# Seven-product steps for two more pairs of K tiles in in1 and o1, blocks opened with a classical step, and squares issued later

## The chip, the cores and the metric

One core of one Trainium2 chip runs the program; it is launched once per measurement. The metric is the device time of one execution in microseconds (us). The kernel before takes 1145.22 us (median of 3 runs, 1143.92 to 1145.31).

## The reference

One layer of an encoder trunk for 256 positions of width 2048, all in float32. What is computed, cut to its products:

```python
n = rmsnorm(h, norm_mix_w)
q_a, k_a, v_a, q_r, k_r, v_r, g_r = split(n @ w_in)     # seven sections of 1024 columns
attn = dilated_mixture_attention(q_a, k_a, v_a)         # 8 heads
ret = bidirectional_retention(q_r, k_r, v_r)            # 8 heads, per-head norm
ret = ret * silu(g_r)
h = h + concat(attn, ret) @ w_out                       # 2048 x 2048
n2 = rmsnorm(h, norm_ffn_w)
h = h + (silu(n2 @ w_gate) * (n2 @ w_up)) @ w_down      # 5632 hidden columns
y = rmsnorm(h, norm_final_w)
```

## The kernel before

**Products.** Each float32 product is made of three products in the format fp32r: an activation and a weight tile are each held as a high and a low half, and high by high, high by low and low by high are accumulated in PSUM (the accumulators beside TensorE). One such matmul has 128 rows of K and 512 columns. ScalarE (ACT) writes a weight tile's high half as a rounded copy, and VectorE (DVE) writes the low half as the difference; both go through the helpers at L156 and L159. A weight tile holds 128 by 1024 numbers and arrives as one DMA of 512 KB that SyncE (SP) issues.

**Blocks.** The program is a row of blocks. A block makes 1024 columns for all 256 positions, in four PSUM banks that are numbered 2, 3, 4 and 8. `in0` to `in6` are the input projection (L787 and L233), `o0` and `o1` the output projection, `gu0` to `gu10` gate and up side by side, and `d0_0`, `d0_1`, `d1_0`, `d1_1`, `d2_0` and `d2_1` the product with `w_down`, which comes after four, eight and eleven `gu` blocks.

**Steps.** A string in `ORDERS` says which steps a block takes and in which order. `C` is the classical step: one weight tile, 12 matmuls. A digit with a letter is one of seven products (Strassen's scheme), which treat two pairs of K tiles together: the letter `a` or `b` names the group, and each digit is 6 matmuls into the bank with that number. A group takes 42 matmuls and four weight loads (three at step 1, one at step 2), where four classical tiles take 48 matmuls. Beside the halves of its tile a seven-product step needs sums of weights: step 1 has VectorE add two loaded tiles into a tile called `rawt` (there is one of it) and GpSimd (POOL) issue an accumulating DMA of 512 KB into `raw12`; step 5 has VectorE add a third tile to `rawt`; step 2 issues another accumulating DMA, from `rawt` into `raw22` (helper `plus`, L178). Steps 3, 5, 6 and 7 also need sums of the activations, `sa_...`, which `pair_sums` makes on VectorE.

**Other letters.** `M` is `mid`: the products 1, 5, 6 and 7 are combined on VectorE into four tiles `part0` to `part3`, one for each quarter of the block's output; the banks 2, 3, 4 and 8 are added to them when their last matmul is done. In `o0` and `o1` the parts are added at `M` into the residual tiles `ht` by four accumulating DMAs of 256 KB on POOL (`add_parts`), and the banks follow as VectorE additions into `ht` (`end_out`). `H`, `T` and `N` are places for other work: `T` transposes (on TensorE, L365) what the block before has made, `H` scales or combines it, and `N` queues work.

**What sets the order.** Each engine runs its instructions in the order in which the program writes them; a manual dependency chains them (`ch`). A weight tile's halves are written three work steps ahead of their products (`AHEAD`), into five buffers `ws`. `later` is a list from which one entry is run behind each work step, `soon` a list that runs behind the next one. So work on VectorE, ScalarE or POOL that waits holds back whatever is written behind it on that engine.

**Around the change.** `sums_n1` queues, for the first two pairs of n1, three entries of `later` each: the sum of the two halves, the sums of its quarters and their halves. Behind them `measure_x` queues 11 entries that fetch x in eight pieces of 256 KB on POOL's queue (L442), and square each on ScalarE three entries later; the sums of these squares give the factor `r1` of the first norm, which `factor` computes on VectorE and POOL (L200 to L202). In the same way `square_ht` squares the eight pieces of `ht` after w_out into `sums_h`, and `gate(gu0)`, which is the `H` of `gu1`, begins with `factor(r2, sums_h)`: with `r2` ScalarE forms the Silu of the gate half and VectorE multiplies the up half (L162), and then `gu0` is transposed into `h2` (`pt_h`). `weighed` writes the halves of a transposed `n2` with the norm's gain, alternating between ScalarE and VectorE.

## Time and profile before

| what | value |
|---|---|
| time, median of 3 runs | 1145.22 us (1143.92 to 1145.31) |
| the profiled execution | 1148.03 us |
| its span, first to last instruction | 1146.2 us |
| granted TensorE clock, mean | 0.995 |
| TensorE (PE) busy | 1127.6 us, 98% |
| VectorE (DVE) busy | 924.2 us, 81% |
| ScalarE (ACT) busy | 681.9 us, 59% |
| GpSimd (POOL) busy | 106.5 us, 9% |

The profile is of one execution. The span is what lies between its first and its last instruction; the remaining 1.8 us of the execution lie around it. Names in the rows are the program's, without the numbers of their buffers: `p_in`, `p_o` and `p_gu` are PSUM banks, `ws_...` weight tiles in halves, `rawc`, `raw12`, `raw22` and `rawt` weight tiles as loaded or summed, `xs` the pieces of x, `pt_...` transposed tiles. "[1.57 <-ACT ws_gu L156]" says that the engine was idle for 1.57 us until an instruction of ScalarE at L156 on that tile released it.

The blocks start on TensorE at these times of the span: `in1` 50.2, `in2` 94.3, `in5` 245.6, `in6` 295.8, `o0` 344.1, `o1` 392.8, `gu0` 437.6, `gu1` 486.0, `gu2` 532.5.

### The profile page before, as it was taken

Reading aid. Unit: us, or ns where it says so; the run is one execution under the profiler, and the core shown is the slowest. Engines: PE = TensorE matmul, PEld = TensorE weight load, DVE = VectorE, ACT = ScalarE, POOL = GpSimd, SP = SyncE. Lnnn points to the kernel's source line nnn. Section 1 sums busy time; section 2 is a strip of 40 time slices with the busy share of each in tenths; the row PEclk is TensorE's granted clock in tenths of the full one; section 3 lists DMA queues with packets and bytes.
Section 4 is the critical chain, followed back from the end, with each engine's and each line's share of the span. In section 5 each row is a group of like instructions: output and inputs, shape, how many; then the busy total and the mean of one; then the engine's idle time right before and its main releaser. Section 6 shows DMA issues by size and latency. Waiting matters only on the chain.

```text
span 1146.2 us, 14428 instructions
## 1 busy us (share of the span) xinstructions
PE 1127.6 (98%) x5166; PEld 935.5 (82%) x5166; DVE 924.2 (81%) x1056; ACT 681.9 (59%) x841; POOL 106.5 (9%) x135
## 2 busy tenths in 40 slices
PE   9999999999999999989999999999999999999996
PEld 7888888888888887878888888888888888888885
DVE  5768876845566868699999878999989977999885
ACT  5675655754656555566666554666666555666653
POOL 0102000000001110010000022000001202000011
PEclk9999999999999999999999999999999999999999
DMA  8969654465588776678898899997898899989795
GB/s 279 308 195 313 209 168 148 150 217 169 174 272 245 218 211 196 208 211 246 261 254 245 258 272 257 284 269 232 251 288 237 229 317 264 277 259 276 240 232 152
DMA packets 78535, 272.03 MB, mean 237 GB/s; under 512 B 9088, under 2 KB 9088, under 8 KB 78464
## 3 DMA queue, kind: packets, MB, share of 16 engines
q1 hardware_dynamic: 61776, 220.76, 55.3%
q0 software_dynamic: 15968, 49.29, 23.1%
q10 hardware_dynamic: 720, 1.07, 0.3%
q8 instruction: 40, 0.66, 0.2%
q14 instruction: 31, 0.25, 0.1%
HBM read 223.90 MB, written 2.10 MB: 197 GB/s over the span
## 4 chain that ended last, share of the span: by engine, by line
PE 83%; DVE 6%; DMA 5%; issue 3%; ACT 2%; POOL 0%; SPq 0%; DVEq 0%; POOLq 0%; ACTq 0%
PE p_gu L233 35%; PE p_in L233 26%; PE p_d L233 13%; PE p_o L233 5%; DMA rawc_d<-in_w_st 2%; DMA rawc_gu<-in_w_st 2%; DVE ws_d L159 2%; DVE ws_gu L159 2%; PE pt_h L365 1%; DMA rawc_o<-in_w_st 1%; DVE ht L159 1%; ACT ws_gu L156 1%; DVE ws_o L159 1%; PE ps_sa L482 1%; PE ps_oa L493 1%
## 5 line engine op out<-in xcount | busy, mean ns | idle before, releaser
L233 PE MATMUL p_gu<-ws_gu,n 128*128 128x512 f32 x1482 | 353.1, 391 | 3.3 <-ACT ws_gu L156 2.6
L233 PEld LDWEIGHTS p_gu<-ws_gu,n 128*128 128x128 f32 x1482 | 278.8, 188 | 62.8 <-ACT ws_gu L156 3.7
L233 PE MATMUL p_in<-ws_in,n 128*128 128x512 f32 x1284 | 302.0, 391 | 1.2 <-ACT ws_in L156 1.1
L233 PEld LDWEIGHTS p_in<-ws_in,n 128*128 128x128 f32 x1284 | 238.2, 188 | 50.4 <-ACT ws_in L156 2.5
L159 DVE TENSOR_TENSOR ws_in<-rawc_in,ws_in 128x1024 fp32r<-128x1024 f32 (+1 forms) x107 | 129.1, 1213 | 62.2 <-ACT ws_in L156 61.3
L233 PE MATMUL p_d<-ws_d,h 128*128 128x512 f32 x708 | 167.9, 389 | 0.4 <-ACT ws_d L156 0.4
L159 DVE TENSOR_TENSOR ws_gu<-rawc_gu,ws_gu 128x1024 fp32r<-128x1024 f32 x113 | 137.8, 1221 | 29.4 <-ACT ws_gu L156 27.6
L233 PEld LDWEIGHTS p_d<-ws_d,h 128*128 128x128 f32 x708 | 132.8, 188 | 28.6 <-ACT ws_d L156 1.1
L156 ACT ACTIVATE ws_in<-rawc_in 128x1024 fp32r<-128x1024 f32 (+1 forms) x107 | 111.6, 1047 | 69.8 <-PE p_in L233 36.1
L156 ACT ACTIVATE ws_gu<-rawc_gu 128x1024 fp32r<-128x1024 f32 x113 | 118.7, 1055 | 56.6 <-DMA rawc_gu<-in_w_st 33.0
L233 PE MATMUL p_gu<-ws_gu,sa_n 128*128 128x512 f32 x504 | 129.3, 392 | 0.0
L233 PEld LDWEIGHTS p_gu<-ws_gu,sa_n 128*128 128x128 f32 x504 | 94.7, 189 | 19.3
L159 DVE TENSOR_TENSOR ws_gu<-raw_gu,ws_gu 128x1024 fp32r<-128x1024 f32 x84 | 102.5, 1220 | 2.2 <-ACT ws_gu L156 1.0
L156 ACT ACTIVATE ws_gu<-raw_gu 128x1024 fp32r<-128x1024 f32 x84 | 88.5, 1054 | 20.9 <-PE p_gu L233 18.5
L159 DVE TENSOR_TENSOR ws_d<-rawc_d,ws_d 128x1024 fp32r<-128x1024 f32 x54 | 65.8, 1221 | 19.1 <-ACT ws_d L156 18.4
L156 ACT ACTIVATE ws_d<-rawc_d 128x1024 fp32r<-128x1024 f32 x54 | 57.1, 1058 | 39.7 <-DMA rawc_d<-in_w_st 22.6
L156 ACT ACTIVATE ws_gu<-rawt_gu 128x1024 fp32r<-128x1024 f32 x42 | 44.3, 1055 | 56.7 <-DVE rawt_gu L159 38.8
L233 PE MATMUL p_d<-ws_d,sa_h 128*128 128x512 f32 x240 | 61.2, 390 | 0.0
L159 DVE TENSOR_TENSOR ws_gu<-rawt_gu,ws_gu 128x1024 fp32r<-128x1024 f32 x42 | 51.3, 1221 | 5.6 <-ACT ws_gu L156 5.6
L233 PEld LDWEIGHTS p_d<-ws_d,sa_h 128*128 128x128 f32 x240 | 44.8, 188 | 9.2
L159 DVE TENSOR_TENSOR ws_d<-raw_d,ws_d 128x1024 fp32r<-128x1024 f32 x40 | 48.8, 1220 | 0.5
L156 ACT ACTIVATE ws_d<-raw_d 128x1024 fp32r<-128x1024 f32 x40 | 42.2, 1055 | 10.5 <-PE p_d L233 9.1
(186 smaller groups left out, 1139.3 us busy)
## 6 DMA issues: line engine op xcount, KB each, us to landing
rawc_gu<-in_w_st SPq DMA_DIRECT2D x113, 512.0 KB, 5.0
rawc_in<-in_w_st SPq DMA_DIRECT2D x105, 512.0 KB, 4.2
raw_gu<-in_w_st SPq DMA_DIRECT2D x63, 512.0 KB, 5.3
rawc_d<-in_w_st SPq DMA_DIRECT2D x58, 512.0 KB, 5.0
raw_d<-in_w_st SPq DMA_DIRECT2D x30, 512.0 KB, 4.7
rawc_o<-in_w_st SPq DMA_DIRECT2D x26, 512.0 KB, 4.8
raw_gu<-raw_gu POOLq DMA_DIRECT2D x21, 512.0 KB, 6.9
raw_gu<-rawt_gu POOLq DMA_DIRECT2D x21, 512.0 KB, 5.3
```

Of the source, the lines that this page charges most:

```text
L156: ch(nc.scalar.activation(out, src, func, **kw))
L159: ch(nc.vector.tensor_tensor(out, x, y, op=op))
L233: ch(nc.tensor.matmul(self.bank(r), x[u], w[v], start=r not in self.begun, stop=self.left[r] == 0))
L365: ch(nc.tensor.transpose(pt[:, f, i * P:(i + 1) * P], t(i)[:, (2 * p + f) * P:(2 * p + f + 1) * P], ident))
L482: ch(nc.tensor.matmul(ps[:, i, :], a, b, start=n == 0, stop=n == 2))
L493: ch(nc.tensor.matmul(ps[:, f, :], a, b, start=i + n == 0, stop=i == 1 and n == 2))
```

## The change

1. `in1` takes a second group of seven products (order string below); its `H`, with the norm's factor and the scaling of `in0`, stands right behind `M`, and its two `T` stand behind one another. Its sums of n1 are made for four pairs where they were made for two, so that `sums_n1` queues twelve entries of `later` ahead of `measure_x`, where it queued six.
2. `in5` becomes a block of kind `in` (one group of seven products); the sums of the first two pairs of n1 are made a second time, by a hook `S` in `in3` and `in4`'s order string, which is filled in `in4`. What `in5` has made is then scaled in the `H` of `in6`.
3. `o1` takes a second group and begins with a classical step; the mixed activations' sums are made for four pairs.
4. `gu0` begins with a classical step.
5. The squares of `ht` are put behind three empty entries of `later` in each of `o0` and `o1`, and `factor(r2, sums_h)` is itself queued in `later` behind the last square, during `gu0`, where it stood at the start of `gate` in `gu1`.
6. `weighed` writes both of ScalarE's copies first, and then both of VectorE's differences.

TensorE gets 5132 matmuls and transposes where it had 5150: three groups more, of 6 matmuls less each. VectorE gets 57 instructions more and ScalarE 16.

```diff
@@ ORDERS @@
-KIND_IN = ("in0", "in1", "in", "in_c", "in_c", "in_c", "in_c")
+KIND_IN = ("in0", "in1", "in", "in_c", "in_c", "in", "in_c")
...
-    "in1": "1a 5a C 2a C 3a C C 6a C 7a M C H C C T C T 4a C C C",
+    "in1": "1a 5a C 2a C 3a C 6a 7a 1b C 4a 5b C 2b 6b C 7b M H C C T T 3b 4b",
     "in": "1a 5a H C 2a C T 3a C T C 6a C 7a M C C C 4a C C C C",
-    "in_c": "C H C T C T C C C C C C C C C C C C C",
+    "in_c": "C H C T C T C C C C C C C S C C C C C C",
     "out0": "1a 5a H C 2a T C 6a 7a M C 3a C 4a C C C C C C C C",
-    "out1": "1a 5a 2a C 3a C T 6a C 7a C M C 4a C T C C C C C C",
-    "gu_first": "1a 5a 2a C T C C T C 3a 6a C 7a C 4a M C C C C C C",
+    "out1": "C 1a 5a 2a C 3a T C C 6a C 7a 1b 4a 5b C 2b 6b C 7b M C T 3b 4b",
+    "gu_first": "C 1a 5a C 2a T C C C T C 3a 6a C 7a C 4a M C C C C",
@@ weighed @@
         for f in range(2):
             copy(to[:, f, 0, :], src[:, f, :], scale=w[:, f:f + 1])
+        for f in range(2):
             stt(to[:, f, 1, :], src[:, f, :], w[:, f:f + 1], to[:, f, 0, :].bitcast(F32), ALU.mult, ALU.subtract)
@@ sums_n1 @@
-    def sums_n1():
-        for p in range(2):
+    def sums_n1(to, n):
+        for p in range(n):
...
-            n1_sums.append(pair_sums(t, f"n1_{p}"))
+            to.append(pair_sums(t, f"n1_{p}"))
@@ attention @@
-            if j < 2:
+            if j < 4:
                 mixed_sums.append(pair_sums(o[0], f"ma{j}"))
@@ the loop over INPUT @@
-            hooks = {"N": [sums_n1, measure_x]}
+            hooks = {"N": [many((sums_n1, n1_sums, 4)), measure_x]}
...
-                hooks = {"H": [many(*([(factor, r1, sums_x)] if b == 1 else []), *([(scaled, prev, 0, 1)] if sec == 0 else []))],
+                hooks = {"H": [many(*([(factor, r1, sums_x)] if b == 1 else []), *([(scaled, prev, 0, 1)] if sec == 0 or half else []))],
...
+            if b == 4:
+                hooks["S"] = [many((sums_n1, n1_again, 2))]
+            end = end_take if b == 0 else end_share if "1a" in ORDERS[KIND_IN[b]] else end_scaled
@@ end_out @@
         tt(o, bank, o, ALU.add)
+        if not block.squares:
+            later.extend([lambda: None] * 3)
+        block.squares += 1
         later.append(lambda: square_ht(sums_h, block.q + n, i))
+        if block.q + block.squares == 6:
+            later.append(lambda: factor(r2, sums_h))
@@ gate @@
-        if block.first:
-            factor(r2, sums_h)
         for i in range(2):
```

The lines of the changed kernel stand one or more lower (L159 is L159 there too, L178 is L179, L233 is L234, L442 is L443). Three places where the order on an engine moves:

**In `in1`, POOL.** `xs00` to `xs31` are the eight pieces of x, `raw12` and `raw22` the accumulating DMAs of the seven products. Before:

```order
L442 DMA xs00_405<-in_x 128x512
L442 DMA xs01_426<-in_x 128x512
L178 DMA raw12_in1_430<-raw22_in1_432 128x1024
L442 DMA xs10_452<-in_x 128x512
L442 DMA xs11_470<-in_x 128x512
L442 DMA xs20_496<-in_x 128x512
L178 DMA raw22_in1_499<-rawt_in1_437 128x1024
L442 DMA xs21_512<-in_x 128x512
L442 DMA xs30_527<-in_x 128x512
L442 DMA xs31_549<-in_x 128x512
```

and changed:

```order
L179 DMA raw12_in1_439<-raw22_in1_441 128x1024
L179 DMA raw22_in1_507<-rawt_in1_446 128x1024
L443 DMA xs00_520<-in_x 128x512
L443 DMA xs01_534<-in_x 128x512
L443 DMA xs10_555<-in_x 128x512
L443 DMA xs11_568<-in_x 128x512
L443 DMA xs20_586<-in_x 128x512
L443 DMA xs21_598<-in_x 128x512
L179 DMA raw12_in1_603<-raw22_in1_605 128x1024
L443 DMA xs30_625<-in_x 128x512
L443 DMA xs31_640<-in_x 128x512
L179 DMA raw22_in1_683<-rawt_in1_610 128x1024
```

The first two pieces stood ahead of group a's DMAs and now stand behind both, and the last two stand behind group b's first DMA, in front of its second.

**In `in1`, ScalarE**, in the middle of the changed block (a `ws` row writes the high half of a weight tile, an `xs` row squares a piece of x):

```order
L156 ACTIVATE ws_in1_630<-rawc_in1_628 128x2x512
L156 ACTIVATE xs20_586,sums_x_93<-xs20_586 128x512
L156 ACTIVATE ws_in1_643<-raw22_in1_507 128x2x512
L156 ACTIVATE xs21_598,sums_x_93<-xs21_598 128x512
L156 ACTIVATE ws_in1_654<-rawt_in1_610 128x2x512
L156 ACTIVATE xs30_625,sums_x_93<-xs30_625 128x512
L156 ACTIVATE ws_in1_667<-rawc_in1_665 128x2x512
L156 ACTIVATE xs31_640,sums_x_93<-xs31_640 128x512
L156 ACTIVATE ws_in1_685<-raw22_in1_683 128x2x512
```

Before, all eight squares stood between the block's second and tenth tile; now the last of them, `xs31`, stands between its fourteenth and its fifteenth, and `xs30`'s stands in front of the fourteenth (`ws_in1_667`, the classical tile behind 5b).

**At the end of `o1`, VectorE**, from `mid` on, before:

```order
L159 TENSOR_TENSOR v_o1_3479<-part0_o1_3475,p6_o1_3404 128x512 [waits Activation_49]
L162 SCALAR_TENSOR_TENSOR part2_o1_3477<-p5_o1_3310,v_o1_3479 128x512 [waits DVE_49]
L159 TENSOR_TENSOR part1_o1_3476<-p7_o1_3445,v_o1_3479 128x512 [waits PE_49]
L159 TENSOR_TENSOR part3_o1_3478<-part2_o1_3477,p7_o1_3445 128x512 [waits DVE_49]
L159 TENSOR_TENSOR ws_o1_3491<-rawc_o1_3489,ws_o1_3491 128x2x512 [waits DMAHW6_49,Activation_49]
L159 TENSOR_TENSOR ws_o1_3508<-rawc_o1_3506,ws_o1_3508 128x2x512 [waits DMAHW7_49,Activation_49]
L159 TENSOR_TENSOR ws_o1_3519<-rawc_o1_3517,ws_o1_3519 128x2x512 [waits DMAHW1_49,Activation_49]
L159 TENSOR_TENSOR ws_o1_3554<-rawc_o1_3552,ws_o1_3554 128x2x512 [waits DMAHW2_49,Activation_49]
L159 TENSOR_TENSOR n2_1_0_3539<-o_n2_10_3540,n2_1_0_3539 128x2x256 [waits Activation_49]
L159 TENSOR_TENSOR n2_1_1_3548<-o_n2_11_3549,n2_1_1_3548 128x2x256 [waits Activation_49]
```

The four additions of banks into `ht` came only with gu0's fourth to sixth tiles there. Changed:

```order
L159 TENSOR_TENSOR v_o1_3681<-part0_o1_3677,p6_o1_3545 128x512 [waits Activation_49]
L162 SCALAR_TENSOR_TENSOR part2_o1_3679<-p5_o1_3413,v_o1_3681 128x512 [waits DVE_49]
L159 TENSOR_TENSOR part1_o1_3678<-p7_o1_3577,v_o1_3681 128x512 [waits PE_49]
L159 TENSOR_TENSOR part3_o1_3680<-part2_o1_3679,p7_o1_3577 128x512 [waits DVE_49]
L159 TENSOR_TENSOR ws_gu0_3693<-rawc_gu0_3691,ws_gu0_3693 128x2x512 [waits DMAHW2_49,Activation_49]
L159 TENSOR_TENSOR ht2_3483<-p2_o1_3382,ht2_3483 128x512 [waits DMASW2_49,PE_49]
L159 TENSOR_TENSOR ht3_3485<-p8_o1_3391,ht3_3485 128x512 [waits DMASW5_49,PE_49]
L159 TENSOR_TENSOR ws_gu0_3734<-rawc_gu0_3728,ws_gu0_3734 128x2x512 [waits DMAHW3_49,Activation_49]
L159 TENSOR_TENSOR rawt_gu0_3737<-rawc_gu0_3728,raw12_gu0_3730 128x1024 [waits DMAHW7_49]
L159 TENSOR_TENSOR ht3_3485<-p3_o1_3385,ht3_3485 128x512 [waits DMASW4_49,PE_49]
L159 TENSOR_TENSOR n2_1_0_3715<-o_n2_10_3716,n2_1_0_3715 128x2x256 [waits Activation_49]
L159 TENSOR_TENSOR n2_1_1_3724<-o_n2_11_3725,n2_1_1_3724 128x2x256 [waits Activation_49]
```

The rows carry the semaphores that they wait for; `DMASW` is one of POOL's DMAs. The additions into `ht` now stand two instructions behind `mid`, and `n2_1_0`, whose high and low halves gu0's first classical step multiplies, stands behind three of them.

More of the change, by code (lines that the diff above doesn't have):

```diff
@@ L410, in end_share @@
         tt(block.share[i, n], bank, block.share[i, n], ALU.add)
-    xt, n1, n1_sums = {}, [], []
+    xt, n1, n1_sums, n1_again = {}, [], [], []
     def fetch_x(p):
@@ L674, in encoder_layer @@
         if sections[0] is not None:
-            prev = Block(f"in{b}", KIND_IN[b], n1, n1_sums, end_take if b == 0 else end_share if b < 3 else end_scaled, hooks,
+            if b == 4:
+                hooks["S"] = [many((sums_n1, n1_again, 2))]
+            end = end_take if b == 0 else end_share if "1a" in ORDERS[KIND_IN[b]] else end_scaled
+            prev = Block(f"in{b}", KIND_IN[b], n1, n1_again if b > 2 else n1_sums, end, hooks,
                          opens=b == 0, early=b < 3)
@@ L707, in encoder_layer @@
         b = Block(f"o{nb}", f"out{nb}", mixed, mixed_sums, end_out, hooks, parts="mid")
-        b.q = 2 * nb
+        b.q, b.squares = 2 * nb, 0
     def gate(block):
-        if block.first:
-            factor(r2, sums_h)
         for i in range(2):
@@ L761, in encoder_layer @@
             b = Block(f"gu{fb}", kind, n2, n2_sums, end_share, hooks)
-            b.first = fb == 0
             def turn_h(b=b, h2=h2, s2=s2, keep=2 * (fb - lo) < s, fb=fb):
```

## The prediction, as made before the result was known

> **What bounds the kernel now.** I read the page first, then the list of waits of TensorE, then busy time in windows that are cut by blocks. The page's first part and the waits:
>
> ```profile
> PE 1127.6 (98%) x5166; PEld 935.5 (82%) x5166; DVE 924.2 (81%) x1056; ACT 681.9 (59%) x841; POOL 106.5 (9%) x135
> ...
> PE pt_h L365 <- DVE part_gu L162: 3.2, 3, 2.6
> PE p_gu L233 <- ACT ws_gu L156: 2.6, 2, 1.6
> PE p_in L233 <- ACT ws_in L156: 1.1, 2, 0.9
> PE p_gu L233 <- DVE ws_gu L159: 0.7, 1, 0.7
> PE p_o L233 <- ACT o_n L156: 0.5, 1, 0.5
> PE p_d L233 <- ACT ws_d L156: 0.4, 1, 0.4
> ```
>
> TensorE is busy 98% of the span, and all its waits for other engines come to some 10 us. So a matmul taken away is time taken away, as long as TensorE finds its next tile ready, and a new wait of it costs its full length. The windows are `in1`, `o1`, `gu0` and, for comparison, `gu2`, a block with two groups of seven products:
>
> ```profile
> 50.20:94.20 44.00, 44.00 (x203) 36.55 (x203) 30.07 (x32) 30.27 (x46) 4.17 (x6) 1.00 0.76 247
> 392.80:437.50 44.70, 44.21 (x203) 36.58 (x202) 32.94 (x48) 26.83 (x41) 3.54 (x5) 1.00 0.72 208
> 437.60:486.00 48.40, 46.14 (x204) 37.50 (x203) 34.74 (x40) 27.50 (x39) 2.50 (x3) 0.96 0.65 204
> 532.50:574.20 41.70, 41.70 (x189) 34.62 (x188) 40.58 (x49) 27.33 (x31) 3.44 (x4) 1.00 0.86 253
> ```
>
> The columns behind the window's length are busy PE, weight loads, DVE, ACT and POOL, then the granted clock. In `in1` and `o1` TensorE is without a gap, or nearly; `gu0` lost 2.3 us and ran at 0.96. A block with two groups asks 40.58 of 41.70 us of VectorE and still leaves TensorE no gap. VectorE has 30 to 33 us of work in `in1` and `o1`, so there is room for a second group on average; what decides is the order in which it and POOL's queue do their work.
>
> **The sum, term by term.** The rows of TensorE for the first four terms, from the chain of waits and the timeline:
>
> ```profile
> 376.61 27.25 PE p_o L233 x120
> 80.33 0.87 PE pt_q L365 x8
> ...
> 405.23 1.66 PE L233 MATMUL p_o<-ws_o,sa_ma 128*128 128x512 f32 x6 [0.49 <-ACT o_n L156]
> 442.05 0.73 PE L233 MATMUL p_gu<-ws_gu,n 128*128 128x512 f32 x2 [0.69 <-DVE ws_gu L159]
> 444.35 4.61 PE L233 MATMUL p_gu<-ws_gu,n 128*128 128x512 f32 x12 [1.57 <-ACT ws_gu L156]
> 495.53 0.33 PE L365 MATMUL pt_h<-ident,part_gu 128*128 128x128 f32 x1 [2.56 <-DVE part_gu L162]
> 496.19 1.76 PE L365 MATMUL pt_h<-ident,part_gu 128*128 128x128 f32 x7 [0.34 <-DVE part_gu L162]
> ```
>
> (1) *Matmuls.* 120 in 27.25 us is 0.227 us for one, 1.36 for a seven-product step and 2.73 for a classical one. Three groups more take 18 matmuls away: **−4.1**.
>
> (2) *o1's T.* Its 6a waited 0.49 for ScalarE, which was held by the copies of the transposed n2. Two classical steps now stand in between: **−0.5**.
>
> (3) *gu0's start.* `gu0` waited 0.69 and 1.57, and after that 12 matmuls took 4.61 instead of 2.73, at a granted clock that the window shows as 0.96. With a classical step first and no accumulating DMA needed at once, both waits and the slow stretch of 1.9 go: **−4.1**. What takes their place is term 8.
>
> (4) *gu1's gate.* The rows of VectorE, POOL and ScalarE there:
>
> ```profile
> 491.64 1.22 DVE L159 TENSOR_TENSOR ws_gu<-raw_gu,ws_gu 128x1024 fp32r<-128x1024 f32 x1
> 493.22 0.72 POOL L202 TENSOR_TENSOR r<-r,mhalf 128x2 f32<-128x2 f32 x1 [3.86 <-DVE r L201]
> 493.97 1.33 ACT L156 ACTIVATE part_gu<-part_gu,r 128x512 f32<-128x512 f32 x2 [6.58 <-POOL r L202]
> 494.73 1.41 DVE L162 SCALAR_TENSOR_TENSOR part_gu<-part_gu,r,part_gu 128x512 f32<-128x512 f32 x2 [1.59 <-ACT part_gu L156]
> ```
>
> With r2 known beforehand ScalarE, idle for 6.58 us, forms the Silus before VectorE is through with its tile at 492.86; the multiplications then start there and not at 494.73, 1.9 earlier. TensorE's wait of 2.56 shrinks to under one, and the 7 transposes behind it, 1.76 us where 8 took 0.87 elsewhere, gain 1.0: **−2.9** (−1 if the slow clock stays and half of the wait, −4 with the rest of it).
>
> (5) *in1, a new wait.* Here the order matters: on POOL the last two pieces of x now stand behind group b's first accumulating DMA, and that waits until VectorE has made group b's `rawt`. ScalarE's square of `xs30` stands in front of the high half of the classical tile behind 5b, so this tile waits for that fetch to land. The rows of `in1`, POOL, then ScalarE, and the times from issue to landing of the fetches at 47.6, at 55.1 and of the two at 27:
>
> ```profile
> 47.08 0.89 POOL L178 DMA_DIRECT2D raw_in<-raw_in  x1 [18.68 <-DVE rawt_in L159]
> 47.64 1.96 POOL L442 DMA_DIRECT2D xs<-in_x  x3
> 54.56 0.90 POOL L178 DMA_DIRECT2D raw_in<-rawt_in  x1 [4.96 <-DVE ws_in L159]
> 55.13 1.97 POOL L442 DMA_DIRECT2D xs<-in_x  x3
> ...
> 61.05 0.63 ACT L156 ACTIVATE xs<-xs 128x512 f32<-128x512 f32 x1 [1.75 <-DMA xs<-in_x]
> 61.67 1.04 ACT L156 ACTIVATE ws_in<-rawc_in 128x1024 fp32r<-128x1024 f32 x1
> ...
> DMA to landing us min/median/max: 6.8/7.0/8.2
> ...
> DMA to landing us min/median/max: 5.9/6.0/6.7
> ...
> DMA to landing us min/median/max: 3.9/4.0/4.0
> ```
>
> Up to 2a the two orders are alike, so `xs00` is issued where a piece was issued before, behind the DMA at 54.56, and its square starts at 61.05 as that one's did. From there a square and a high half take 0.62 + 0.95 = 1.57; 6a's and 7a's tiles go ahead and 1b's high half ends at 65.8. VectorE writes the low half (1.22) and adds `rawt` (as long, 1.14 start to start): 68.2. POOL issues the accumulating DMA at 68.5, and by the row at 47.64, 0.56 behind such a DMA and 6.8 to land, `xs30` is there 7.4 later, at 75.9. Square and high half: 77.6. TensorE starts `in1` at 50.2; nine seven-product steps and four classical ones, 23.2, bring it to that tile at 73.4. Wait: **+4.2**; with the fetch at 4.0, as at 27, 1.4; with 8.2, 5.6. An idle time of 2.3 in `gu0` was followed by the slow stretch, so I add the same **+1.9** (0 to 1.9).
>
> [...]
>
> (6) *The end of in1 and in2's start.* `M H C C T T 3b 4b` brings the scaling and four transposed halves together. Rows of ScalarE from the groups of 70 to 95:
>
> ```profile
> L156 ACT ACTIVATE part_in<-part_in,r 128x512 f32<-128x512 f32 x4 | 2.6, 711 | 3.7 <-POOL r L202 3.7
> L156 ACT ACTIVATE q<-pt_q 128x512 fp32r<-128x512 f32 x2 | 1.1, 576 | 0.0
> ```
>
> From the end of 7b: VectorE's `mid` and the factor 1.8, POOL 0.8, four scalings 2.6, two high halves 2.0 (7.2); VectorE's low half and `rawt` of in2's first group 2.5 (9.7); ScalarE's half of `rawt` 1.05, four transposed halves 2.3 and the first classical tile of `in2` 1.05 (14.1). TensorE wants that one after two classical steps, 16 transposes (1.7) and four seven-product steps: 12.6. That is 1.5 late; VectorE's low half, behind four additions, a sum and four halves more, is another 1.5 late: **+3.0** (0 to 4).
>
> (7) *in5.* Its second step uses sums that VectorE finishes behind `in4`'s scaled copies: **+0.4** (0 to 1); the rest of the moved work lies in blocks where VectorE has 30 us of 44.
>
> (8) *o1's end, the largest term.* VectorE's additions of banks 2 and 8 into `ht2` and `ht3` now stand two instructions behind `mid`, and the second waits for the fourth accumulating DMA. Behind it stand gu0's 1a tile, its `rawt`, another addition and then the low half of `n2_1_0`, which gu0's first step multiplies. Rows of `o1` now, VectorE, POOL, and the landing of those DMAs; the last row is that of the same three DMAs at 1124, of `d2_1`:
>
> ```profile
> 416.27 0.68 DVE L159 TENSOR_TENSOR part_o<-part_o,p_o 128x512 f32<-128x512 f32 x1
> 416.87 2.36 DVE L159 TENSOR_TENSOR ws_o<-rawc_o,ws_o 128x1024 fp32r<-128x1024 f32 x2
> ...
> L178 POOL DMA_DIRECT2D ht<-part_o x3: 862/1221/1579, 416.7 to 417.7; - x3
> DMA to landing us min/median/max: 5.3/8.0/10.0
> ...
> DMA to landing us min/median/max: 3.3/4.3/5.2
> ```
>
> From the end of 7b: two combinations at 0.68, 1.35; the last DMA issued 0.8 behind (417.7 against 416.95), 2.15; landing 10.0 as here, 12.15. Then two additions at 0.6 start to start, two tiles (2.36) and the half of `n2_1_0` (0.68): 4.24, together 16.4. TensorE wants it after a classical step, 16 transposes and 3b, 4b, that is 2.73 + 1.74 + 2.72 = 7.2. Wait: **+9.2**, and the slow stretch, **+1.9**. With 5.2, the longest landing at 1124, it is 4.4. I take the upper row since it is of the very place, when `o1`'s weights use the same DMA engines. What is hidden behind the wait before, eight classical steps (22 us), is what the new order gives up.
>
> Sum: −4.1 − 0.5 − 4.1 − 2.9 + 6.1 + 3.0 + 0.4 + 11.1 = **+9.0**. The profiled execution, 1148.0 us with 1146.2 of span, would be 1157; it lies 2.8 above the median of the runs, so on the median's footing the forecast is 1145.2 + 9.0 = **1154 us**.
>
> **The rivals.** Some 0.2%, 2.3 us, is what a measurement here can tell from no change.
>
> *A. The forecast*, chance 0.52. Its own range is 1147 to 1160: term 8 without its slow stretch and at 5.2 gives 1147.5, term 5 at 5.6 and term 6 at 4 give 1156.6, and some more for what isn't seen.
>
> *B. VectorE is late at 7b of o1*, 0.10. Rows of `o1`, TensorE's 7a and VectorE's first combination:
>
> ```profile
> 409.46 1.52 PE L233 MATMUL p_o<-ws_o,sa_ma 128*128 128x512 f32 x6
> 414.35 0.68 DVE L159 TENSOR_TENSOR v_o<-part_o,p_o 128x512 f32<-128x512 f32 x1
> ```
>
> VectorE reached `mid` 3.4 us after 7a's end at 410.98. With a second group there it may be as late again, and then term 8 is longer by 3.4: 1157.6. Against it: `gu2`, with two groups, has no wait on VectorE.
>
> *C. Only one of the two large waits is there*, 0.16. Without term 5 the sum is +2.9 (1148.1), without term 8 it is −2.1 (1143.1). For it speaks that each hangs on one landing. Most of it, 0.13, falls within 0.2%.
>
> *D. The other side: POOL's transfers land as quickly as its quickest rows*, 0.22. One mechanism: both waits stand on the time from issue to landing, and they decide only if it is over some 2.6 us in `in1` and 0.8 at o1's end (for the one 7.4 less 4.2, less 0.6; for the other 10.0 less 9.2). [...] Against it: the quick rows are of other places; those of `in1` itself are 5.9 to 8.2, and of the three at o1's end one is 5.3 and the longest 10.0.
>
> [...]
>
> **How the numbers follow.** Faster: D, 0.22. Same: C's 0.13. Slower: A, B and the rest of C, 0.65. The range 1140 to 1160 leaves out about 0.1 on either side: D with short terms 6 and 7, and A or B with long landings.
>
> **What would show it.** Right: in the list of TensorE's waits one of 3 to 6 us on ScalarE at `ws_in` in `in1`'s second half, with ScalarE waiting for `xs` just before; one of 4 to 9 us on VectorE at `n2` at gu0's start, with VectorE waiting for a DMA into `ht`; gu1's wait on `part_gu` below 1; a clock under 1 behind the two long ones. Wrong: VectorE reaching gu0's first tile in time, which ends term 8 and makes the change faster; a wait elsewhere, above all at o1's 7b or in `in5`; or gu1's wait unchanged, if r2 itself is late.

## The result and the profile after

The changed kernel takes 1162.34 us (median of 5 runs, 1161.42 to 1163.48) against 1145.22 us for the kernel before (median of 5, 1143.92 to 1147.33): 1.0136 times the time, with a 95% interval of 1.0115 to 1.0156, or 13 to 18 us more. The prediction had the side right and the size wrong: 1154 us, with a range that ended at 1160.

The profiled execution of the changed kernel has a span of 1160.6 us, 14.4 more than that of the kernel before, whose own profiled execution was 2.8 above its median.

The first part of the page of the changed kernel, and the whole list of TensorE's waits (us in total, times, longest):

```profile
PE 1128.7 (97%) x5148; PEld 934.6 (81%) x5148; DVE 957.5 (83%) x1113; ACT 695.5 (60%) x857; POOL 112.6 (10%) x141
...
PE p_in L234 <- ACT ws_in L156: 9.2, 3, 4.6
PE p_gu L234 <- DVE n L159: 8.8, 1, 8.8
PE p_in L793 <- POOL zero L125: 1.3, 1, 1.3
PE ps_sa L483 <- ACT part_in L156: 1.2, 1, 1.2
PE p_in L234 <- DVE part_in L159: 1.0, 2, 0.7
PE p_in L234 <- DVE ws_in L159: 0.9, 1, 0.9
PE p_d L234 <- ACT ws_d L156: 0.4, 1, 0.4
```

Busy PE hardly moved (1128.7 us for 1127.6), although 18 matmuls are gone (5148 records of TensorE here, 5166 before), since some of the rest became slower. The two waits that the prediction named are the first two rows; but the first one is two long waits, not one. TensorE's timeline at the three long waits, and at gu1's transposes:

```profile
68.28 5.25 PE L234 MATMUL p_in<-ws_in,sa_n 128*128 128x512 f32 x12 [4.60 <-ACT ws_in L156]
84.37 7.08 PE L234 MATMUL p_in<-ws_in,n 128*128 128x512 f32 x18 [4.01 <-ACT ws_in L156]
460.42 5.90 PE L234 MATMUL p_gu<-ws_gu,n 128*128 128x512 f32 x14 [8.80 <-DVE n L159]
513.51 1.03 PE L366 MATMUL pt_h<-ident,part_gu 128*128 128x128 f32 x8
```

Each wait is followed by a slow stretch: 12 matmuls in 5.25 us instead of 2.73 (2.5 more), 18 in 7.08 instead of 4.09 (3.0), 14 in 5.90 instead of 3.18 (2.7), all reckoned at 0.227 us a matmul. The last row has no wait any more.

The time from a block's first product on TensorE to the next block's, worked out from TensorE's rows for all blocks (`in0` begins with the matmuls on `zero`), says where the 14.4 us are. Beside it stands what the prediction's terms make of each block:

| block | before | changed | difference | predicted |
|---|---|---|---|---|
| in1 | 44.0 | 57.2 | +13.2 | −1.4 + 6.1 = +4.7 |
| in2 | 46.2 | 50.3 | +4.1 | +3.0 |
| in5 | 50.2 | 49.1 | −1.1 | −1.4 + 0.4 = −1.0 |
| o1 | 44.7 | 42.6 | −2.1 | −1.4 − 0.5 = −1.9 |
| gu0 | 48.4 | 55.5 | +7.1 | −4.1 + 11.1 = +7.0 |
| gu1 | 46.5 | 41.7 | −4.8 | −2.9 |
| in0 | 48.9 | 48.6 | −0.3 | 0 |
| in3, in4, in6, o0 | 202.2 | 202.2 | 0 | 0 |
| gu2 to d2_0 | 573.5 | 572.0 | −1.5 | 0 |

`in5`, `o1` and `gu0` came out within some 0.2 us of the forecast. `in1` missed by 8.5 us, more than the whole miss of 5.4 (14.4 for 9.0): `gu1` and the blocks from `gu2` on gave 1.9 and 1.5 back, and for the latter the change gives no reason. In `in1` ScalarE and POOL show what happened. The rows are ScalarE's at the two long waits, POOL's, and the times from issue to landing of the six pieces of x issued at 55.3 and of the two at 74.6:

```profile
66.56 0.63 ACT L156 ACTIVATE xs<-xs 128x512 f32<-128x512 f32 x1 [10.55 <-DMA xs<-in_x]
82.65 0.63 ACT L156 ACTIVATE xs<-xs 128x512 f32<-128x512 f32 x1 [6.61 <-DMA xs<-in_x]
...
54.74 0.87 POOL L179 DMA_DIRECT2D raw_in<-rawt_in  x1 [6.47 <-DVE ws_in L159]
55.28 3.57 POOL L443 DMA_DIRECT2D xs<-in_x  x6
74.05 0.89 POOL L179 DMA_DIRECT2D raw_in<-raw_in  x1 [15.20 <-DVE rawt_in L159]
74.61 1.43 POOL L443 DMA_DIRECT2D xs<-in_x  x2
...
DMA to landing us min/median/max: 11.3/13.4/13.9
...
DMA to landing us min/median/max: 8.0/8.1/8.1
```

The first piece was issued at 55.28, where the forecast had 55.13, but landed 11.3 us after that, not 5.9. ScalarE stood still for 10.55 us in front of its square, and 6a's tile, which is next on ScalarE, reached TensorE 4.6 us late. What was on the DMA engines then, in the list of issues between 52 and 62 (KB each, median us to landing), of the kernel before:

```profile
rawc_in<-in_w_st SPq DMA_DIRECT2D x2, 512.0 KB, 5.9
xs<-in_x POOLq DMA_DIRECT2D x3, 256.0 KB, 6.0
raw_in<-rawt_in POOLq DMA_DIRECT2D x1, 512.0 KB, 5.8
```

and of the changed one:

```profile
rawc_in<-in_w_st SPq DMA_DIRECT2D x3, 512.0 KB, 10.0
raw_in<-in_w_st SPq DMA_DIRECT2D x3, 512.0 KB, 7.5
xs<-in_x POOLq DMA_DIRECT2D x6, 256.0 KB, 13.4
raw_in<-rawt_in POOLq DMA_DIRECT2D x1, 512.0 KB, 10.5
```

That is 2304 KB before and 5120 KB now, 2.2 times as much, and the pieces of x take 13.4 us in place of 6.0 in the median, the first one 11.3 in place of 5.9. That both medians and bytes grew 2.2 times is no law: with the window to 67 the bytes are 1.8 times as many. The weight tiles, on SyncE's queue, became slower too (`rawc_in` 10.0 us for 5.9 in the median). So did the accumulating DMA that stands in front of the pieces in POOL's queue, 10.5 us for 5.8. The next view is the busy time in the windows 58 to 64 and 64 to 70 (the last two columns are the busy share of the DMA engines and GB/s), of the changed kernel:

```profile
58.00:64.00 6.00, 5.69 (x26) 4.37 (x24) 0.00 (x0) 0.00 (x0) 0.85 (x2) 1.00 1.00 291
64.00:70.00 6.00, 1.72 (x4) 1.43 (x5) 1.40 (x2) 3.44 (x7) 0.00 (x0) 0.69 1.01 401
```

The DMA engines are full for these 12 us (1.00 and 1.01), and from 58 to 64 neither VectorE nor ScalarE does anything. In the kernel before the DMA engines were full to 64 (0.98), then at 0.56.

At o1's end the profile is the one that was forecast. VectorE, and the landing of the four accumulating DMAs into `ht`:

```profile
451.21 0.69 DVE L159 TENSOR_TENSOR ht<-p_o,ht 128x512 f32<-128x512 f32 x1 [3.56 <-DMA ht<-part_o]
456.21 0.69 DVE L159 TENSOR_TENSOR ht<-p_o,ht 128x512 f32<-128x512 f32 x1 [4.31 <-DMA ht<-part_o]
459.69 1.28 DVE L159 TENSOR_TENSOR n<-o_n,n 128x512 fp32r<-128x512 f32 x2
...
DMA to landing us min/median/max: 6.6/7.9/8.8
```

VectorE waits 3.56 and 4.31 us for the DMAs, and the low half of `n2_1_0` comes right before TensorE's row at 460.42.

### The profile page after: what moved, and what is told of

Its sections match the earlier page's. It is cut to its first block, busy times and chain, and to the rows that moved or that the text cites. A ratio compares the mean times of both kernels' runs of the same rounds, so it can differ in the third digit from the quotient of the medians.

```text
span 1160.6 us, 14498 instructions
## 1 busy us (share of the span) xinstructions
PE 1128.7 (97%) x5148; PEld 934.6 (81%) x5148; DVE 957.5 (83%) x1113; ACT 695.5 (60%) x857; POOL 112.6 (10%) x141
## 4 chain that ended last, share of the span: by engine, by line
PE 73%; DMA 9%; issue 8%; DVE 6%; ACT 2%; POOL 1%; SPq 0%; DVEq 0%; POOLq 0%; ACTq 0%
PE p_gu L234 38%; PE p_in L234 17%; PE p_d L234 13%; DMA rawc_in<-in_w_st 3%; DMA rawc_d<-in_w_st 2%; DVE ws_in L159 2%; DMA xs<-in_x 2%; PE p_o L234 2%; DVE ws_d L159 1%; ACT ws_in L156 1%; DMA rawc_gu<-in_w_st 1%; PE pt_h L366 1%; DMA ht<-part_o 1%; DVE ht L159 1%; DVE ws_gu L159 1%
## 5 line engine op out<-in xcount | busy, mean ns | idle before, releaser
L234 PE MATMUL p_gu<-ws_gu,n 128*128 128x512 f32 x1482 | 353.7, 391 | 8.9 <-DVE n L159 8.8
L234 PEld LDWEIGHTS p_gu<-ws_gu,n 128*128 128x128 f32 x1482 | 279.6, 189 | 68.2 <-DVE n L159 9.2
L234 PE MATMUL p_in<-ws_in,n 128*128 128x512 f32 x1224 | 292.5, 394 | 6.7 <-ACT ws_in L156 4.6
L234 PEld LDWEIGHTS p_in<-ws_in,n 128*128 128x128 f32 x1224 | 228.6, 190 | 56.7 <-ACT ws_in L156 7.7
L234 PE MATMUL p_d<-ws_d,h 128*128 128x512 f32 x708 | 167.8, 389 | 0.4 <-ACT ws_d L156 0.4
L159 DVE TENSOR_TENSOR ws_gu<-rawc_gu,ws_gu 128x1024 fp32r<-128x1024 f32 x113 | 138.0, 1221 | 25.9 <-ACT ws_gu L156 24.0
L159 DVE TENSOR_TENSOR ws_in<-rawc_in,ws_in 128x1024 fp32r<-128x1024 f32 (+1 forms) x101 | 122.0, 1211 | 44.0 <-ACT ws_in L156 43.2
L234 PEld LDWEIGHTS p_d<-ws_d,h 128*128 128x128 f32 x708 | 132.8, 188 | 28.4 <-ACT ws_d L156 1.0
L156 ACT ACTIVATE ws_in<-rawc_in 128x1024 fp32r<-128x1024 f32 (+1 forms) x101 | 105.6, 1047 | 54.1 <-DMA rawc_in<-in_w_st 27.2
L234 PE MATMUL p_gu<-ws_gu,sa_n 128*128 128x512 f32 x504 | 128.5, 391 | 0.0
L234 PEld LDWEIGHTS p_gu<-ws_gu,sa_n 128*128 128x128 f32 x504 | 94.0, 188 | 19.1
L159 DVE TENSOR_TENSOR ws_gu<-raw_gu,ws_gu 128x1024 fp32r<-128x1024 f32 x84 | 102.5, 1220 | 1.9 <-ACT ws_gu L156 0.6
L159 DVE TENSOR_TENSOR ws_d<-rawc_d,ws_d 128x1024 fp32r<-128x1024 f32 x54 | 65.8, 1221 | 17.8 <-ACT ws_d L156 17.2
L234 PE MATMUL p_d<-ws_d,sa_h 128*128 128x512 f32 x240 | 61.2, 390 | 0.0
L159 DVE TENSOR_TENSOR ws_gu<-rawt_gu,ws_gu 128x1024 fp32r<-128x1024 f32 x42 | 51.3, 1221 | 4.2 <-ACT ws_gu L156 4.1
L234 PEld LDWEIGHTS p_d<-ws_d,sa_h 128*128 128x128 f32 x240 | 44.8, 188 | 9.2
L156 ACT ACTIVATE ws_d<-raw_d 128x1024 fp32r<-128x1024 f32 x40 | 42.2, 1056 | 13.2 <-PE p_d L234 12.0
L159 DVE TENSOR_TENSOR ws_d<-raw_d,ws_d 128x1024 fp32r<-128x1024 f32 x40 | 48.8, 1219 | 0.7
```

The lines of the kernel that those rows point to most:

```text
L156: ch(nc.scalar.activation(out, src, func, **kw))
L159: ch(nc.vector.tensor_tensor(out, x, y, op=op))
L234: ch(nc.tensor.matmul(self.bank(r), x[u], w[v], start=r not in self.begun, stop=self.left[r] == 0))
```

## The experiments

Theory: the loss is two transfers that land late in front of an engine that the program chains in order (`ch`), the pieces of x in `in1` and the accumulating DMAs at o1's end. Rivals: the weight tiles are what is late in `in1`; VectorE has too much to do at o1's end; the two losses depend on each other. The times of the kernel before in these comparisons were taken beside each experiment, and lie between 1145.2 and 1147.8 us, so ratios are compared, and beside them the blocks.

**The squares later.** The fetches stay, each square comes six entries behind its fetch instead of three.

```diff
-        for n in range(11):
-            later.append(lambda n=n: (n < 8 and fetch(*divmod(n, 2)), n > 2 and take()))
+        for n in range(14):
+            later.append(lambda n=n: (n < 8 and fetch(*divmod(n, 2)), n > 5 and take()))
```

> The changed kernel with one edit: each piece of x is squared six entries of the list later than it is fetched, where it was three; the fetches stay where they are. Theory (the fetches land late, and the squares that wait for them hold back ScalarE's high halves): TensorE's waits of 4.6 and 4.0 us in in1 fall below 0.5 each and the two stretches of slow matmuls behind them, some 2.4 us each, go with them, so some 13 us less than the changed kernel: 1149 us. Rival (the weight tiles themselves arrive late in in1, because a second group and the fetches share the DMA engines): the waits stay, on the loads, and the time is over 1158.

Measured: 1152.38 us, 1.0041 of the kernel before (1.0024 to 1.0059); the changed kernel had 1.0136, so 11 us of its loss are gone. `in1` takes 45.6 us instead of 57.2. TensorE's waits:

```profile
PE p_gu L234 <- DVE n L159: 8.6, 1, 8.6
...
PE p_in L234 <- ACT ws_in L156: 0.9, 3, 0.5
```

Both long waits in `in1` are gone, though the landings are as long (10.0 to 14.5 us for the eight pieces): the loads of the weights were not what TensorE waited for. `in2` still takes 50.2.

**o1's parts on VectorE.**

```diff
+            if self.parts == "dve":
+                for (i, n), t in self.share.items():
+                    o = ht[self.q + n][:, i]
+                    tt(o, t, o, ALU.add)
             if self.parts == "mid":
                 self.add_parts()
...
-        b = Block(f"o{nb}", f"out{nb}", mixed, mixed_sums, end_out, hooks, parts="mid")
+        b = Block(f"o{nb}", f"out{nb}", mixed, mixed_sums, end_out, hooks, parts="dve" if nb else "mid")
```

> The changed kernel with one edit: in o1 the four parts are added to the residual by four more additions on VectorE behind mid, in place of POOL's four accumulating DMAs. Theory (VectorE stands still for the last accumulating DMA): no DMA has to land; VectorE has 2.4 us more to do, so gu0's first step comes about 2.5 us late instead of 8.8, with a shorter slow stretch or none: 6 to 9 us less than the changed kernel, 1153 to 1156. Rival (VectorE has too much work at o1's end, the landing doesn't matter): four more additions make the wait 2.4 longer, 1165.

Measured: 1156.59 us, 1.0069 (1.0045 to 1.0094), some 8 us less than the changed kernel by the ratios. `gu0` takes 49.5 us instead of 55.5, and its wait is this row, in place of 8.8:

```profile
PE p_gu L234 <- DVE n L159: 3.6, 1, 3.6
```

VectorE does four additions more, and the wait is 5.2 us shorter. So the landing was the larger part of it, and the rival, by which the wait would have grown, is out. The wait is not all landing: the four additions take 2.49 us (446.86 to 449.35), so by an estimate 1.1 us of the 3.6 would be left without them, for VectorE's other work there.

**Both, and o1's second T earlier.**

```diff
-    "out1": "C 1a 5a 2a C 3a T C C 6a C 7a 1b 4a 5b C 2b 6b C 7b M C T 3b 4b",
+    "out1": "C 1a 5a 2a C 3a T C T C 6a C 7a 1b 4a 5b C 2b 6b C 7b M C 3b 4b",
```

> The changed kernel with both edits, the squares six entries behind and o1's parts on VectorE, and o1's second T moved ahead of 6a, one step behind the first, so that gu0's first tile of n2 is done long before mid. Theory: none of the three long waits of TensorE is left, nor the slow stretches: 1162.3 less 13 less 11 is 1138, faster than the kernel before by 7, which is what the removed matmuls (4.1), o1's T, gu0's start and gu1's gate were to bring (11.6), less some 2 to 4 in in2. Rival (the waits come back at other places, as VectorE has over 33 us of work in o1 now): between 1141 and 1150.

Measured: 1149.44 us, 1.0015 (1.0001 to 1.0029): not 7 us faster than the kernel before but 2 slower. The rival held. `in1` is at 45.5 us, but `in2` at 50.0 and `gu0` at 53.3, where the second experiment had 49.5. In the list of waits the one of 8.8 has become several, on other tiles:

```profile
PE p_gu L234 <- ACT n L156: 1.9, 1, 1.9
PE p_gu L234 <- ACT ws_gu L156: 1.6, 1, 1.6
PE p_gu L234 <- DVE n L162: 0.8, 1, 0.8
```

The first and the third lie at gu0's T, in front of the products with the tile that it transposed. What held ScalarE there is a weight tile, whose row stands right ahead of the copies of that tile:

```profile
461.31 1.06 ACT L156 ACTIVATE ws_gu<-rawc_gu 128x1024 fp32r<-128x1024 f32 x1 [4.79 <-DMA rawc_gu<-in_w_st]
```

So this is a third transfer that lands late in front of such an engine: the weight tile was issued at 453.66 and landed 7.5 us later, beside POOL's accumulating DMA of 452.79. In the changed kernel ScalarE waits at the same place, for 3.53 us, but its copies are done 2 us before TensorE comes to the tile.

**The second T earlier, alone.** The last diff by itself.

> The changed kernel with one edit: o1's second T stands one step behind the first, ahead of 6a, so that the low half of gu0's first tile of n2 no longer stands behind the additions into the residual. Theory (VectorE stands still until the fourth accumulating DMA has landed, whatever is behind it): the wait moves to the next instruction behind it, the low half of gu0's 1a tile, and to 5a's: some 4 and 2 us, in place of 8.8, so 2 to 4 us less than the changed kernel. Rival (what was wrong is the place of n2's half alone): the wait goes, 9 to 11 us less.

Measured: 1166.60 us, 1.0170 (1.0144 to 1.0195): not 2 to 4 us less than the changed kernel but, by the ratios, some 4 more. The intervals of the two touch; `gu0` alone, at 59.7 us in place of 55.5, makes it 4.2. The wait did move to the next tile behind the additions, as the theory says, but the sum is larger, not smaller.

```profile
PE p_gu L234 <- DVE ws_gu L159: 5.5, 1, 5.5
PE p_gu L234 <- ACT n L156: 1.8, 1, 1.8
PE p_gu L234 <- ACT ws_gu L156: 1.6, 2, 1.1
PE p_gu L234 <- DVE ht L159: 1.2, 1, 1.2
PE p_gu L234 <- DVE n L162: 0.8, 1, 0.8
```

The expectation left out two things: TensorE also waits for the bank that the additions into `ht` are to free (1.2), and the wait at gu0's T is there again, with ScalarE idle for 5.17 us before a weight tile. That explains some 4 us of the third experiment's miss, which is 9 by the ratios: o1's earlier T, or what comes of it, costs that much in `gu0` (53.3 against 49.5, and 59.7 against 55.5). Beside that, `gu0` is at 49.5 even without it, where terms 1 to 4 reckoned with 44.3, and `in1` at 45.5, where they reckoned with 42.6. Why the weight tile lands late with the earlier T wasn't tried.

**in1 alone.** The kernel before, with in1's new order string and the sums for four pairs.

```diff
-    "in1": "1a 5a C 2a C 3a C C 6a C 7a M C H C C T C T 4a C C C",
+    "in1": "1a 5a C 2a C 3a C 6a 7a 1b C 4a 5b C 2b 6b C 7b M H C C T T 3b 4b",
...
-        for p in range(2):
+        for p in range(4):
             t = ttile(f"xw_{p}")
```

> The kernel before with the second group of in1 alone (its order string and sums of n1 for four pairs, so that all fetches of x move into in1). Theory: in1 alone brings the two waits (8.6), their slow stretches (4.9) and in2's waits (1.9 to 3), less 6 matmuls (1.4): 1145.2 plus 14 is 1159. Rival (the waits come from in1 together with another part of the change): under 1150.

Measured: 1160.19 us, 1.0106 (1.0080 to 1.0132), some 12 us more than the kernel before, so in1 needs no other part of the change for its loss. `in1` takes 55.2 us and `in2` 50.1, with the waits of the changed kernel, 2.9 and 5.2 us where that had 4.6 and 4.0:

```profile
PE p_in L233 <- ACT ws_in L156: 8.7, 3, 5.2
```

**in1 taken back.** The changed kernel with in1's old order string and sums for two pairs.

> The changed kernel with in1 taken back to one group. Theory (in1 and o1's end are two losses with nothing in common): the changed kernel's 17.1 over the kernel before, less the 12.4 that in1 alone cost: 4 to 5 us slower than the kernel before, with o1's wait of 8.8 in place. Rival (the two hang together, for instance by what in1's end leaves on the queues): above 8 or below 2.

Measured: 1146.83 us, 1.0003 (0.9988 to 1.0019). That is below the expected 4 to 5 us, and below the 2 that the rival named: everything else in the change costs nothing in sum. `o1` (42.6), `gu0` (55.7, with a wait of 9.2), `in5` (49.0) and `gu1` (41.7) are as in the changed kernel. By the blocks, −2.1 + 7.2 − 1.2 − 4.8 is −0.9, which agrees; so the blocks do not bear the rival out. In1 alone (1.06% more) and the rest alone (0.03%) come to 1.09%, against 1.36% with an interval from 1.15: with their intervals the two losses may simply add, and a connection isn't shown.

**in5 alone.** The kernel before with part 2 of the change.

```diff
-KIND_IN = ("in0", "in1", "in", "in_c", "in_c", "in_c", "in_c")
+KIND_IN = ("in0", "in1", "in", "in_c", "in_c", "in", "in_c")
...
-    "in_c": "C H C T C T C C C C C C C C C C C C C",
+    "in_c": "C H C T C T C C C C C C C S C C C C C C",
...
+            if b == 4:
+                hooks["S"] = [many((sums_n1, n1_again, 2))]
```

> The kernel before with part 2 of the change alone: in5 takes one group of seven products, and in4's hook makes the sums of the first two pairs of n1 anew. Theory: six matmuls of 0.227 us less, nothing waits: 1.4 us less than the kernel before. Rival (the second set of sums and the scaling in in6 hold VectorE back): a wait of TensorE in in5 or in6, and no gain.

Measured: 1145.66 us, 0.9989 (0.9971 to 1.0008), too close to the kernel before for the runs to tell. The block does tell: `in5` takes 49.0 instead of 50.2, with no wait, 1.2 us less where 1.4 was expected.

**One group in in1 and in o1.** The changed kernel with both order strings and both numbers of sums taken back.

> The changed kernel with in1 and o1 taken back to one group each (their order strings and numbers of sums as before). What is left of the change: in5's group, gu0's classical first step, the squares and r2 earlier, and weighed's order. Theory (each of these brings what the prediction's terms 1, 3 and 4 say, and all that was lost is in1's and o1's): 1.4 + 4.1 + 2.9 = 8.4 us less than the kernel before on the same chip, the fastest of all. Rival (gu0's start or gu1's gate still waits): less than 4 us.

Measured: 1144.16 us, 0.9974 (0.9952 to 0.9995), faster than the kernel before by some 3 us, not 8. gu1 is at 41.7 and in5 at 49.0, as expected; `gu0` is at 49.1, not better than the 48.4 before, with a new wait:

```profile
PE p_gu L234 <- DVE ht L159: 3.3, 1, 3.3
```

This is the bank for 1a: the additions that free it are written behind the tiles for gu0's first three steps. So the prediction's term 3, −4.1, was no gain of its own here: a wait on ScalarE and VectorE gave way to one on a bank.

**Two classical steps first.** The last kernel with one step moved.

```diff
-    "gu_first": "C 1a 5a C 2a T C C C T C 3a 6a C 7a C 4a M C C C C",
+    "gu_first": "C C 1a 5a 2a T C C C T C 3a 6a C 7a C 4a M C C C C",
```

> The kernel with in1 and o1 taken back to one group each, and gu0 beginning with two classical steps in place of one (C C 1a 5a 2a T ...). In the kernel with one such step TensorE still waited 3.3 us at gu0's start, for the bank that VectorE's additions into the residual were to free; these stand behind the tiles prepared for the next three steps, 1a, 5a and their two sums among them. Theory: with two classical steps first they stand behind 1a's tile and one sum alone, some 2.4 us earlier, and TensorE needs the bank 2.7 us later: no wait and no slow matmuls at gu0's start, 3.3 + 1.4 = some 4 to 5 us less than that kernel, 7 to 9 less than the kernel before. Rival (another wait follows, on ScalarE's half of 5a's sum): within 2 us of the kernel with one classical step.

Measured: 1145.39 us, 0.9995 (0.9977 to 1.0013): no gain, and by the ratios 2.4 us more than with one such step, with intervals that overlap. The theory's 4 to 5 us did not come. Another wait did follow, as the rival says, though not on 5a's sum alone: the wait for the bank is gone, and in its place come one at gu0's T, where ScalarE is again idle before a weight tile (6.38 us), and others:

```profile
PE p_gu L234 <- ACT n L156: 1.6, 1, 1.6
PE p_gu L234 <- DVE n L162: 0.8, 1, 0.8
PE p_gu L234 <- DVE ws_gu L159: 0.7, 1, 0.7
```

**The pieces of x through SyncE's queue.**

```diff
-            ch(nc.gpsimd.dma_start(got[-1][2], x[q][:, i]))
+            ch(nc.sync.dma_start(got[-1][2], x[q][:, i]))
```

> The changed kernel with one edit: the pieces of x are fetched through SyncE's queue in place of POOL's, at the same place of the program. Theory A (what makes the fetches late is that all sixteen DMA engines are full, with two accumulating DMAs, six fetches and the weight tiles of two groups at once): the first piece still takes 8 us or more to land, the waits of 4.6 and 4.0 us stay within 1.5 us in sum, and the time is that of the changed kernel within 3 us. Theory B (POOL's queue is the slow part): the pieces land within 5 us, both waits go, and the time is 10 to 13 us less than the changed kernel.

Measured: 1149.02 us, 1.0019 (1.0000 to 1.0039), some 13 us less than the changed kernel. By the time theory B held; by the landings neither did in full, since B wanted them within 5 us and A the first one at 8 or more:

```profile
L443 SPq DMA_DIRECT2D xs<-in_x x8: 327/414/598, 41.0 to 56.6; - x8
DMA to landing us min/median/max: 7.5/10.2/12.2
```

The pieces took 7.5 to 12.2 us here too, so slow landings were not confined to POOL's queue. But SyncE's queue does not stand behind the accumulating DMAs: the first piece was issued at 41.0, 14 us earlier, and the last at 56.6, and ScalarE waited for none of them. `in1` took 43.3 us, the least of all. So the run moved the time of issue as well, which neither theory had reckoned with. With landings nearly as long the waits are gone, so the late issue was a cause too: on POOL's queue the pieces stand behind an accumulating DMA that itself waits for VectorE.

**Half of x.** Only the first 256 columns of each piece of 512 are fetched and squared, so that the norm's factor leaves out half of x.

```diff
-            ch(nc.gpsimd.dma_start(got[-1][2], x[q][:, i]))
+            ch(nc.gpsimd.dma_start(got[-1][2][:, :S], x[q][:, i][:, :S]))
...
-            square(o, o, accum_out=sums_x[:, i, q:q + 1])
+            square(o[:, :S], o[:, :S], accum_out=sums_x[:, i, q:q + 1])
```

> The changed kernel with one edit: only the first half of each piece of x is fetched and squared, 128 KB in place of 256; the norm's factor leaves out the other half, so this computes something else. Theory A (landing is bytes outstanding over what the DMA engines move): 0.8 MB less of some 3 MB that stand ahead of or beside the first piece, so it lands after 8 to 9 us in place of 11.3; the wait at 6a falls from 4.6 to some 2 us and the second one by 1 to 2 us. Theory B (a fixed time for each DMA on POOL's queue, behind the accumulating one): the landings stay at 11 us, and both waits too.

Measured, in one execution: 1157.17 us, and `in1` 52.3 instead of 57.2. The landings of the six pieces, and TensorE's waits in `in1`:

```profile
DMA to landing us min/median/max: 9.9/10.6/11.2
...
PE p_in L234 <- ACT ws_in L156: 5.9, 3, 3.1
```

The waits are 2.1 and 3.1 in place of 4.6 and 4.0. These numbers also differ between executions that fetch all of x with POOL's DMAs in this order, the changed kernel and five of the experiments. There the median landing of the six pieces was 12.2 to 13.4 us, the first piece's 10.1 to 11.3, and that of the accumulating DMA in front 9.2 to 10.5; the waits, where the squares stand as in the changed kernel, were 2.9 to 4.7 and 4.0 to 5.2. So the pieces that stand behind others did land sooner with half the bytes (10.6 in the median), as theory A says. But 9.9 for the first piece is hardly outside that scatter, 9.8 for the DMA in front is within it, and 768 KB less of 5120 did not bring the first piece to the 8 to 9 us expected. What delayed the first piece, the weight tiles, that DMA or both, one execution can't tell.

**What is worth keeping.** The changed kernel with in1's old order string and sums for two pairs, and o1's parts on VectorE.

> The changed kernel with in1 taken back to one group and o1's parts added on VectorE. Theory (the losses lie in in1 with in2's start and in gu0's wait for the accumulating DMAs, and add up block by block): from one TensorE block start to the next in1 takes 44 to 46 us and in2 46.3, as with the old in1, o1 42.6, gu0 49.5, gu1 41.7, in5 49.0, which is 5 to 7 us less than the kernel before in sum. Rival (with in1 quick the rest shifts): gu0 over 52 us, and no more than 2 us less than the kernel before.

Measured: 1140.78 us, 0.9960 (0.9946 to 0.9974), 4 to 5 us less than the kernel before, the lowest ratio of all (the interval overlaps that of the kernel with one group in both). `o1` 42.6, `gu1` 41.7 and `in5` 49.1 are as expected; `gu0` took 50.2, and `in1` 46.7 and `in2` 47.3 in the profiled execution, in which ScalarE waited 2.26 us for one of in1's fetches; that is a little less gain than the 5 to 7 us of the theory. The waits of TensorE in those two blocks:

```profile
PE p_gu L234 <- DVE n L159: 3.2, 1, 3.2
PE p_in L234 <- ACT ws_in L156: 1.9, 1, 1.9
```

## Why the prediction was right or wrong

**Terms 1, 2 and 7** were right in `in5` and `o1`: −1.1 for −1.0, −2.1 for −1.9. In `in5` that is in part luck: nothing waits there, so term 7's 0.4 was not there, and the six matmuls brought 1.1 to 1.2, not 1.4.

**Terms 3 and 8, together, were right**: +7.1 in `gu0` for +7.0, and the wait is 8.8 for 9.2, of the named instruction. The landing was 8.8, not 10.0. The second experiment shows the cause by taking the DMAs away. That the size came out so well is partly luck. The low half was ready 1.0 us sooner than the forecast had it, by the shorter landing, but TensorE also wanted it 0.6 us sooner: the forecast counted 16 transposes in o1's T, and there are 8. And the slow stretch was 2.7, not 1.9. Term 3's −4.1, as a gain by itself, is not shown: where term 8's cause was taken away, `gu0` still took 49.1 to 50.2 us (53.3 with o1's earlier T), against 48.4 before. Nor is the slow stretch of 1.9 in it regular. `in5 alone` has the old start of `gu0` and the same two waits, and no slow stretch behind them, where the kernel before took 4.61 us for these 12 matmuls:

```profile
446.95 3.03 PE L233 MATMUL p_gu<-ws_gu,n 128*128 128x512 f32 x12 [1.57 <-ACT ws_gu L156]
```

**Term 4** had the right sign and was too small: −4.8 for −2.9. gu1 now takes 41.7 us, what gu2 takes. The two waits, 2.9 us, are gone whole, and besides the slow transposes the products behind them had been slow as well, some at 0.427 us. The kernel before isn't always that late: with the same gate, `in1 alone` and `in5 alone` had 43.4 and 43.6 in `gu1`, so the gain lies between 1.7 and 4.8 us, by the execution it is measured against.

**Term 6** named the place, and was 1 us too small: +4.1 in `in2` for +3.0. Of the two waits it was made of, ScalarE's first classical tile, 1.5, is not in the list, and VectorE's low half is 0.9 and not 1.5. The others it did not name: 0.3 and 0.7 for VectorE's additions into `part_in`, and 1.2 in front of the scores of attention, for ScalarE's `part_in`. Some 1 us, by an estimate from the block's sum, is slower products around them: behind the wait of 0.71 eight took 2.50 us, behind that of 0.93 eight took 2.10. So its size came out nearly right by other waits than its own. in2's loss stays when in1's long waits are gone (the block takes 49.9 to 50.3 in all eight kernels with in1's second group).

**Term 5 is where it failed.** The step reads: "`xs00` is issued where a piece was issued before, behind the DMA at 54.56, and its square starts at 61.05 as that one's did." The place of issue was right to 0.15 us; the square started at 66.56. The price of a landing was taken from a row with three pieces behind one accumulating DMA. In the changed kernel there are six pieces, and six weight tiles instead of two. So a whole wait was missed, which the sum had at nothing: 4.6 us at 6a and 2.5 of slow matmuls behind it. That the late landing in front of ScalarE makes both waits is shown: they go when the squares stand further behind the fetches, and when the fetches are issued 14 us earlier. Why the first piece took 11.3 us is less settled: more bytes were under way, the DMA engines were full (1.00 and 1.01 from 58 to 70), and the accumulating DMA in front took 4.7 us longer itself, but which of these counts for how much stays open. The second wait, where the step worked forward from that square, was 4.0 for 4.2, and that is luck: TensorE came to that tile 7.0 us later than forecast and the piece landed 6.7 later (5.5 in the issue, 1.2 in a landing of 8.0 for 6.8), so the subtraction came out alike. Of the 8.5 us by which `in1` missed, 7.1 are the first wait and its slow stretch.

**Rivals.** B (VectorE late at o1's 7b) did not come: o1 shows no wait. C and D did not come either; D's condition, quick landings on POOL's queue, is the very thing that failed on the other side: in `in1` the landings were 8.0 to 13.9 us. To come out faster D also needs short waits to leave no slow stretch behind them, and no run shows that they do so each time: a slow stretch followed 1.57 us in the kernel before, and none the same wait in `in5 alone`.

## What to carry to other kernels

The time from issue to landing did not stay with the DMA here: a piece that had landed in 5.9 us took 11.3 behind the same DMA, with 2.2 times the bytes issued around it. So read it together with all that is issued around it, on every queue, and do not carry it over to an order that puts more there. Before an instruction that waits for a transfer is moved in the order of an engine that feeds the critical one, ask what stands behind it, and either put it several steps further behind its issue, issue the transfer sooner, or take it out; all three worked here (`in1` at 45.6 and 43.3 us for 57.2, `gu0` at 49.5 for 55.5). And a wait that was removed at gu0's start gave way to the next one in three kernels (a bank in one, with 3.3 us; the tile behind gu0's T in two, with 1.9 and 1.6), so look for what is ready next before such a wait is booked as a gain.

## What the runs showed of the hardware

- Slow matmuls, at 0.427 us instead of 0.227, stood behind waits of TensorE, but not behind each. In the kernel before 8 of them followed the wait of 1.57 us, and behind that of 2.56 seven transposes took 1.76 us; in the changed kernel 10 to 12 followed each of the waits of 4.01, 4.60 and 8.80 us, and none those of 0.93 and 1.24. In the experiments they followed waits of 1.99 us (`in5 alone`), 2.07 (half of x) and 2.86 (`in1 alone`), and did not follow the one of 1.57 in `in1 alone` and `in5 alone`, nor one of 1.94 in `in1` of the last kernel. How many they were did not go by the wait: 5 behind 8.59 us (squares later), 12 behind 3.18 (the last kernel).
- The kernel before has a chance of such a wait of its own. `in5 alone` leaves in1 as it was, and its profiled execution has a wait of ScalarE for a piece of x, as the change made it regular, with TensorE waiting 1.99 us behind it; the rows are ScalarE's, and the landing of in1's three pieces at 48.7:

```profile
57.28 0.63 ACT L156 ACTIVATE xs<-xs 128x512 f32<-128x512 f32 x1 [3.54 <-DMA xs<-in_x]
...
DMA to landing us min/median/max: 8.5/9.3/10.2
```

  The kernel before's row has 6.8/7.0/8.2 there, and no wait. `in1` takes from 43.9 to 47.8 us in the kernels with the old order string, while `in3`, `in4`, `in6` and `o0`, without such fetches, repeat to 0.1 us. This may be a good part of why the kernel before scatters between 1141 and 1153 us over 25 runs, but that was not tried.
